# A hybrid decoder layer on one core: TensorE's order written out at two seams, after the recurrence and at attention's last head

## The chip, the cores and the metric

The kernel runs on one core of a Trainium2 chip. The time is the device time of one execution in microseconds (us); the figures given are medians of several executions. Five engines work side by side, each through its own list of instructions in order: TensorE (PE: products and transposes; its weight loads are shown as PEld), VectorE (DVE), ScalarE (ACT), GpSimd (POOL) and SyncE (SP), which issues most DMAs. They wait for one another by semaphores.

## The reference: what is computed

One layer of a decoder, 512 tokens of width 1024, all in float32:

```python
h    = rms_norm(x, norm_g)
proj = h @ w_in     # recurrence q, f, i and gate z_a; attention c_q, c_kv, rope key, gate z_b; merge gates
y_a  = hgrn2_branch(hq, hf, hi, hz, lb, hg_norm_g)   # 8 heads of 128, chunkwise gated recurrence,
                                                     # per-head rms_norm, * silu(z_a)
y_b  = mla_branch(cq, ckv, kr, mz, ...)              # 8 heads, latent attention: 128 plain + 64 rotated
                                                     # dimensions per key, causal softmax, * silu(z_b)
g    = sigmoid(glog + b_gate)
x    = x + (g[0] * (y_a @ w_proj_a) + g[1] * (y_b @ w_proj_b)) @ w_out
out  = rms_norm(x, final_norm_g)
```

## The kernel before

**Products.** Every large product is done as three products of rounded operands (`mm3`, lines 90 to 92): high x high, high x low, low x high. Each operand is therefore first split into a high half (a copy on ScalarE) and a low half (a subtraction on VectorE): weights in `load_w` (L111, L112), other operands in `split` (L149, L150). `proj_ch` projects 256 channels of `w_in` for all tokens: two weight halves `kh`, for each two groups of 128 channels `m`, for each four blocks `k`, that is 48 products of 128x512.

**Memory.** TensorE writes to PSUM. Of its eight banks the pool `mm` has three (projections) and the pool `ax` five (everything else: scores, states, outputs, transposes).

**Stages.** After the latent projections, the recurrence goes through its heads in four pairs (`hg_pair`). A pair projects the forget gate, the values or the output gate, and the query, then per head: `hg_states` (transposes L487, copy L488 to `kt`, products L492, VectorE L493 and L496), `hg_scores` (L504, L509, L512, then a masked copy L513 to `asb`), `hg_out` (L523, L525, then squares L529 on ScalarE, a power on GpSimd, L154 and L155, and the scaling L531 on VectorE into a buffer named `k128`), and `hg_gate` (transposes L539, then L540 into `ya`).

In the last pair two pieces of attention are written in between: `before_gate` does `mla_rope(0)` and `mla_nope(0)`, and `before_out` does `mla_scores(0)`, ahead of `hg_out`. Then comes `mla_gate(0)` (24 products on `hT`), and last `finish()`, which is `hg_gate` of both heads.

`mla_rope` makes the rotated query: a projection, a copy to `qr` (L598), DMAs that swap its halves (L600), three GpSimd operations (L601 to L603), a second pair of DMAs that exchanges the partition halves (L607), a rounding copy (L609) and a subtraction into `qp` (L613). `mla_nope` makes the plain query and key. `mla_scores` goes through four blocks of 128 queries; in each it issues

```python
mm3(sps[:, :n], qn, kn, ...)                                        # plain part, 3 products
for x in range(2):
    nc.tensor.matmul(sps[:, :n], qh[:, bl], kpe[x][:, :n], ...)     # rotated part, L658
```

and then the softmax (L661 to L666) into `p`. `mla_transpose` turns `p` by ten transposes (L679) and splits it into `pt`; `mla_out` multiplies it with the values and the result with the gate `z` (L689).

The loop over attention's heads does, for the next head ahead of time, the scores, gate and projections. At the last head it projects the first merge gates (`gates(0, 0)`: 48 products and two activations L698), then transposes, and after the loop comes `mla_out`. The merge follows: `parts` splits `ya` (eight copies on ScalarE, eight subtractions on VectorE), and `proj_ch` multiplies it with `w_proj_a`.

**Order.** Nearly all of the order is made by a planner: it takes the instructions in the order in which they are written as their priority, runs a time model of the engines, and writes down for each engine a fixed list. The engines then run these lists as they are. Only the start of the kernel is in a `tc.manual_schedule` block, in which the named engines keep the written order. `tc.issue_after(ins)` puts what is issued inside it on the engine of `ins` behind `ins` in that engine's list; before, the splitting of `ya` on ScalarE stands behind the last exponential of the last head (`last_exp`).

Of the kernel before, what the change touches and what calls it, by code (L numbers as in the profile page):

```python
# [13 lines left out]
AF = mybir.ActivationFunctionType  # L14
# [5 lines left out]
D = 1024  # L20
# [3 lines left out]
H = 8  # L24
# [3 lines left out]
COL_G = COL_ZB + 1024  # L28
# [10 lines left out]
def hybrid_layer(ctx: ExitStack, tc: tile.TileContext, a):  # L39
    nc = tc.nc  # L40
# [76 lines left out]
        v = mat[:, c0 : c0 + w].rearrange("(k p) c -> p k c", p=P)  # L117
        return [load_w(v[:, 4 * i : 4 * i + 4, :]) for i in range(2)]

    def proj_ch(mat, c0, rhs):  # L120

        ps = [mm_tile() for _ in range(2)]
        for kh, w in enumerate(load_cols(mat, c0)):
            for m in range(2):
                for k in range(4):
                    kk = 4 * kh + k
                    mm3(ps[m][:], w, rhs, (slice(None), k, slice(m * P, m * P + P)),
                        (slice(None), kk), kk == 0, kk == KD - 1)
        return ps

    def proj_tok(mat, c0, lhs, done):
# [3 lines left out]
        for t2 in range(NT // 2):  # L135
# [8 lines left out]
            for t in range(2):  # L144
                done(2 * t2 + t, ps[t])

    def split(hi, lo, src):

        nc.scalar.copy(hi, src)  # L149
        nc.vector.tensor_tensor(lo, src, hi.bitcast(F32), op=ALU.subtract)  # L150

    def power(out, x, mul, add, expo):
# [346 lines left out]
    def hg_scores(h, ki, ko, k64, qi, q64):  # L499

        asb, aps = asb_[h % 2], ax_tile()
        for i in range(NT):
            b = slice(i * P, i * P + P)
            nc.tensor.matmul(aps[:, b], ki[:, b], qi[:, b], start=True, stop=True)  # L504

        for c in (0, 2):
            for i in range(NT):
                blk = lambda n: slice(i * P + n * C, i * P + n * C + C)
                nc.tensor.matmul(aps[c * C : c * C + C, blk(c + 1)], ko[:, blk(c)], qi[:, blk(c + 1)], start=True, stop=True)  # L509
        for i in range(NT):  # L510
            b = slice(i * 64, i * 64 + 64)
            nc.tensor.matmul(aps[0:64, i * P + 64 : i * P + P], k64[:, b], q64[:, b], start=True, stop=True)  # L512
        nc.vector.copy_predicated(asb[:].rearrange("p (g t) -> p g t", g=NT),  # L513
                                  mask_le[:].rearrange("p (o t) -> p o t", o=1).broadcast_to([P, NT, P]),
                                  aps[:].rearrange("p (g t) -> p g t", g=NT))
        return asb

    def hg_out(h, asb, st_, q128, v_sb):

        ops = ax_tile()  # L520
        for i in range(NT):
            sl = slice(i * P, i * P + P)
            nc.tensor.matmul(ops[:, sl], asb[:, sl], v_sb[i][:, (h % 4) * P : (h % 4) * P + P], start=True, stop=i == 0)  # L523
            if i:
                nc.tensor.matmul(ops[:, sl], q128[:, sl], st_[:, i * P - P : i * P], start=False, stop=True)  # L525
        ss, on = W("ss", 2, (P, NT)), W("k128")
        for i in range(NT):
            osq = W("osq", 1, (P, P))
            nc.scalar.activation(osq[:], ops[:, i * P : i * P + P], AF.Square, accum_out=ss[:, i : i + 1])  # L529
        power(ss[:], ss[:], 1.0 / P, 4 * EPS, neg_half)  # L530
        nc.vector.tensor_tensor(on[:].rearrange("p (g v) -> p g v", g=NT), ops[:].rearrange("p (g v) -> p g v", g=NT),  # L531
                                ss[:].rearrange("p (g o) -> p g o", o=1).broadcast_to([P, NT, P]), op=ALU.mult)
        return on
# [12 lines left out]

    v_sb = [None] * NT

    def hg_pair(pair, before_gate=None, before_out=None):
        cc, hs = pair * 256, (2 * pair, 2 * pair + 1)  # L550
        pf = proj_ch(w_in, COL_F + cc, hT)
        kk = [hg_forget(h, pf[i]) for i, h in enumerate(hs)]
        def gate():
            pz = proj_ch(w_in, COL_ZA + cc, hT)
            zz = [z_tile() for _ in hs]
            for i in range(2):
                silu2(zz[i][:], pz[i][:])
            return zz

        if pair % 2 == 0:  # L560
            for t in range(NT):
                v_sb[t] = hw.tile([P, 512], F32, f"v{t}")
            proj_tok(w_in, COL_I + cc, hT, lambda t, ps: nc.scalar.copy(v_sb[t][:], ps[:]))
        else:
            zz = gate()
        pq = proj_ch(w_in, COL_Q + cc, hT)
        qq = [hg_query(h, pq[i], kk[i][0]) for i, h in enumerate(hs)]
        sts = [hg_states(h, kk[i][5], kk[i][1], v_sb) for i, h in enumerate(hs)]
        if before_gate:
            before_gate()  # L570
        if pair % 2 == 0:
            zz = gate()
        aa = [hg_scores(h, kk[i][2], kk[i][3], kk[i][4], qq[i][0], qq[i][1]) for i, h in enumerate(hs)]
        if before_out:
            before_out()
        on = [hg_out(h, aa[i], sts[i], qq[i][2], v_sb) for i, h in enumerate(hs)]

        def finish():
            for i, h in enumerate(hs):
                hg_gate(h, on[i], zz[i])  # L580
        return finish

    w_uq = a["w_uq"][0].rearrange("(k p) (h c) -> p k h c", p=P, h=H)
# [51 lines left out]
    def mla_gate(h):  # L637
        w = load_w(w_in[:, COL_ZB + h * P : COL_ZB + h * P + P].rearrange("(k p) c -> p k c", p=P))
        ps = mm_tile()
        for k in range(KD):  # L640
            mm3(ps[:], w, hT, (slice(None), k), (slice(None), k), k == 0, k == KD - 1)
        z = z_tile()
        silu2(z[:], ps[:])
        return z

    last_exp = [None]

    def mla_scores(h, pool, qn, kn, qp, final=False):

        pn = []  # L650
        for i in range(NT):
            n = (i + 1) * P
            bl = slice(i * P, n)
            sps = ax_tile()
            qh = qp[h % 2]
            mm3(sps[:, :n], qn, kn, (slice(None), bl), (slice(None), slice(0, n)), True, False)
            for x in range(2):
                nc.tensor.matmul(sps[:, :n], qh[:, bl], kpe[x][:, :n], start=False, stop=x == 1)  # L658
            sm = pool.tile([P, 4], F32, "sm", 4)
            p = pool.tile([P, n], F32, f"p{i}")  # L660
            nc.vector.tensor_tensor(sps[:, bl], sps[:, bl], mask_inf[:], op=ALU.add)  # L661
            nc.vector.tensor_reduce(sm[:, 0:1], sps[:, :n], axis=AX.X, op=ALU.max, negate=True)
            nc.vector.tensor_scalar(sm[:, 1:2], sm[:, 0:1], SCALE, None, op0=ALU.mult)  # L663
            last_exp[0] = nc.scalar.activation(p[:, :n], sps[:, :n], AF.Exp, scale=SCALE, bias=sm[:, 1:2], accum_out=sm[:, 2:3])  # L664
            nc.vector.reciprocal(sm[:, 3:4], sm[:, 2:3])
            (nc.vector if final else nc.gpsimd).tensor_scalar(p[:, :n], p[:, :n], sm[:, 3:4], 0.5, op0=ALU.mult, op1=ALU.mult)  # L666
            pn.append(p)
        return pn
# [15 lines left out]
    def mla_out(h, pts, v, z):  # L684
        ops = mm_tile()
        for j in range(NT):
            mm3(ops[:, j * P :], v, pts[j], (slice(None), j, slice((h % 4) * P, (h % 4) * P + P)), (slice(None),),
                j == 0, j == NT - 1)
        nc.vector.tensor_tensor(yb[:, h], ops[:], z[:], op=ALU.mult)  # L689


    def gates(b, c):

        res = []
        for i, ps in enumerate(proj_ch(w_in, COL_G + b * D + c * 256, hT)):
            j = 8 * b + 2 * c + i
            g = z_tile()
            nc.scalar.activation(g[:], ps[:], AF.Tanh, scale=0.5, bias=hb_gate[:, j : j + 1])  # L698
            res.append(g)
        return res  # L700

    for pair in range(H // 2 - 1):
        hg_pair(pair)()
    early = []

    def first_scores():
        early.append(mla_rope(0))
        early.append(mla_nope(0, ma_pool))

    finish = hg_pair(H // 2 - 1, first_scores, lambda: early.append(mla_scores(0, ma_pool, *early[1], early[0])))  # L710
    z = mla_gate(0)
    finish()
    hw.close()

    mw = Pool("mla", "right")
# [4 lines left out]
    for h in range(H):  # L720
        pools = (ma_pool, mw)
        if h:
            pn = mla_scores(h, pools[h % 2], *nope, qp, h + 1 == H)
        if h + 1 < H:
            if h % 2:
                qp = mla_rope((h + 1) // 2)
        if h:
            z = mla_gate(h)
        if h + 1 < H:
            nope = mla_nope(h + 1, pools[(h + 1) % 2])  # L730
        if late:
            mla_out(*late)
        if h % 4 == 0:
            v = mla_values(h)
        hook = lambda: mla_transpose(pn)
        if h + 1 == H:
            first_gates = gates(0, 0)
            pts = hook()
        else:
            pts = hook()  # L740
        late = (h, pts, v, z)
    mla_out(*late)
    mw.close()
    ma_pool.close()
    cpool.close()
# [11 lines left out]
    mp = Pool("merged", "right")  # L757
    ma = mp.tile([P, KD, S], F32, "ma")
    yap = Pool("ya_parts", "right")
    with tc.issue_after(last_exp[0].ins):  # L760
        yas = parts(yap, ya, "ya")
    for c in range(4):
        for i, (g, ps) in enumerate(merge(0, c, yas, a["w_proj_a"][0], None if c else first_gates)):
# [109 lines left out]
```

## Time and profile before

| | |
|---|---|
| time, median of 3 | 641.39 us (640.81 to 641.47) |
| the profiled execution | 641.92 us, its span 640.1 us |
| TensorE busy | 624.4 us (98%) |
| VectorE, ScalarE, GpSimd busy | 354.3, 238.9, 114.9 us |
| mean granted clock of TensorE | 0.991 |
| waits of TensorE for L531 and for `pt` | 3.4 us in two, 2.3 us in one |

The profile is of one execution. "Busy" of TensorE is modelled from pipelined instructions. The granted clock is the share of full speed that the chip gave TensorE in a stretch. In the lists of instructions a row has the start, the duration, the engine, the line, the operation, the output and inputs by their names, their shapes, and in brackets how long the engine had been idle before and what ended that.

### The profile page before, as it was taken

Reading aid. Unit: us, or ns where it says so; the run is one execution under the profiler, and the core shown is the slowest. Engines: PE = TensorE matmul, PEld = TensorE weight load, DVE = VectorE, ACT = ScalarE, POOL = GpSimd, SP = SyncE. Lnnn points to the kernel's source line nnn. Section 1 sums busy time; section 2 is a strip of 40 time slices with the busy share of each in tenths; the row PEclk is TensorE's granted clock in tenths of the full one; section 3 lists DMA queues with packets and bytes.
Section 4 is the critical chain, followed back from the end, with each engine's and each line's share of the span. In section 5 each row is a group of like instructions: output and inputs, shape, how many; then the busy total and the mean of one; then the engine's idle time right before and its main releaser. Section 6 shows DMA issues by size and latency. Waiting matters only on the chain.

```text
span 640.1 us, 8392 instructions
## 1 busy us (share of the span) xinstructions
PE 624.4 (98%) x3204; PEld 525.4 (82%) x3204; DVE 354.3 (55%) x552; ACT 238.9 (37%) x451; POOL 114.9 (18%) x213
## 2 busy tenths in 40 slices
PE   8999999999999999979999999989999999999995
PEld 5998888888888888868888888878888888888884
DVE  7727855497944478567567756556322342434244
ACT  5554241333242232355445645344222232323223
POOL 3106200332401033231213141000000010111011
PEclk9999999999999999999999999989999999999998
DMA  7425153133124103411332243123332323334403
GB/s 258 139 66 177 34 165 99 33 90 108 34 69 129 46 23 97 120 33 52 90 95 71 54 141 89 34 66 93 102 85 91 101 89 100 99 98 155 175 10 122
DMA packets 58808, 59.75 MB, mean 93 GB/s; under 512 B 5736, under 2 KB 52238, under 8 KB 58768
## 3 DMA queue, kind: packets, MB, share of 16 engines
q1 hardware_dynamic: 56492, 55.54, 28.9%
q10 hardware_dynamic: 2132, 3.15, 1.7%
q8 instruction: 25, 0.41, 0.3%
q0 software_dynamic: 144, 0.52, 0.3%
q14 instruction: 15, 0.12, 0.1%
HBM read 55.01 MB, written 2.10 MB: 89 GB/s over the span
## 4 chain that ended last, share of the span: by engine, by line
PE 95%; DVE 2%; ACT 1%; issue 0%; DMA 0%; POOL 0%; POOLq 0%; DVEq 0%; ACTq 0%
PE mm_ps L90 26%; PE mm_ps L92 26%; PE mm_ps L91 25%; PE ax_ps L90 2%; PE ax_ps L92 2%; PE ax_ps L91 2%; PE ax_ps L658 2%; PE ax_ps L679 2%; PE mm_ps L260 1%; PE ax_ps L504 1%; PE ax_ps L523 1%; PE ax_ps L492 1%; PE ax_ps L512 1%; PE ax_ps L525 1%; PE ax_ps L539 1%; PE ax_ps L509 1%
## 5 line engine op out<-in xcount | busy, mean ns | idle before, releaser
L112 DVE TENSOR_TENSOR w_lo<-w_raw,w_hi 128x1024 fp32r<-128x1024 f32 (+3 forms) x90 | 108.9, 1213 | 129.8 <-ACT w_hi L111 128.4
L111 ACT CAST w_hi<-w_raw 128x1024 fp32r<-128x1024 f32 (+3 forms) x90 | 89.3, 995 | 175.5 <-PE mm_ps L91 124.6
L90 PE MATMUL mm_ps<-hT,w_hi 128*128 128x512 f32 x384 | 150.6, 393 | 0.0
L91 PE MATMUL mm_ps<-hT,w_hi 128*128 128x512 f32 x384 | 149.9, 390 | 0.0
L92 PE MATMUL mm_ps<-hT,w_lo 128*128 128x512 f32 x384 | 149.3, 391 | 0.0
L92 PEld LDWEIGHTS mm_ps<-hT,w_lo 128*128 128x128 f32 x384 | 72.1, 188 | 14.8
L91 PEld LDWEIGHTS mm_ps<-hT,w_hi 128*128 128x128 f32 x384 | 72.1, 188 | 14.5
L90 PEld LDWEIGHTS mm_ps<-hT,w_hi 128*128 128x128 f32 x384 | 72.2, 188 | 14.3
L774 POOL TENSOR_TENSOR ma<-ma,z 128x512 f32<-128x512 f32 x8 | 11.8, 1480 | 181.1 <-DVE z L773 181.1
L91 PE MATMUL mm_ps<-w_lo,hT 128*128 128x512 f32 (+1 forms) x96 | 36.5, 382 | 0.0
L92 PE MATMUL mm_ps<-w_hi,hT 128*128 128x512 f32 (+1 forms) x96 | 36.4, 382 | 0.0
L90 PE MATMUL mm_ps<-w_hi,hT 128*128 128x512 f32 (+1 forms) x96 | 36.4, 386 | 0.0
L666 POOL TENSOR_SCALAR p<-p,sm 128x128 f32<-128x128 f32 (+3 forms) x28 | 16.9, 605 | 81.9 <-DVE sm L663 73.7
L449 DVE RECIPROCAL tf<-pr 128x512 f32<-128x512 f32 x8 | 26.8, 3349 | 0.2
L664 ACT ACTIVATE p<-ax_ps,sm 128x128 f32<-128x128 f32 (+3 forms) x32 | 16.9, 529 | 26.6 <-DVE sm L663 26.5
L91 PE MATMUL mm_ps<-ya,w_hi 128*128 128x512 f32 x64 | 25.7, 402 | 0.0
L92 PE MATMUL mm_ps<-ya,w_lo 128*128 128x512 f32 x64 | 25.6, 399 | 0.0
L90 PE MATMUL mm_ps<-ya,w_hi 128*128 128x512 f32 x64 | 25.5, 398 | 0.0
L90 PE MATMUL mm_ps<-yb,w_hi 128*128 128x512 f32 x64 | 24.9, 389 | 0.0
L91 PE MATMUL mm_ps<-yb,w_hi 128*128 128x512 f32 x64 | 24.9, 389 | 0.0
L92 PE MATMUL mm_ps<-yb,w_lo 128*128 128x512 f32 x64 | 24.9, 389 | 0.0
L150 DVE TENSOR_TENSOR wo<-wo_raw,wo 128x1024 fp32r<-128x1024 f32 x8 | 9.6, 1224 | 25.9 <-ACT wo L149 25.9
(226 smaller groups left out, 1124.6 us busy)
## 6 DMA issues: line engine op xcount, KB each, us to landing
w_raw<-w_in SPq DMA_DIRECT2D x58, 512.0 KB, 3.9
w_raw<-w_proj_a SPq DMA_DIRECT2D x8, 512.0 KB, 3.4
w_raw<-w_proj_b SPq DMA_DIRECT2D x8, 512.0 KB, 3.3
wo_raw<-w_out SPq DMA_DIRECT2D x8, 512.0 KB, 3.4
xr<-x SPq DMA_DIRECT2D x4, 512.0 KB, 7.7
w_raw<-w_in SPq DMA_DIRECT2D x4, 448.0 KB, 4.7
x<-x SPq DMA_DIRECT2D x3, 512.0 KB, 8.4
w_raw<-w_uq SPq DMA_DIRECT2D x8, 192.0 KB, 2.7
```

Source lines behind the costliest of these rows:

```text
L90: nc.tensor.matmul(ps, lh[lsl], rh[rsl], start=start, stop=False)
L91: nc.tensor.matmul(ps, lh[lsl], rl[rsl], start=False, stop=False)
L92: nc.tensor.matmul(ps, ll[lsl], rh[rsl], start=False, stop=stop)
L111: nc.scalar.copy(hi[:, :o], raw[:, :o])
L112: (lo_eng or nc.vector).tensor_tensor(lo[:, :o], raw[:, :o], hi[:, :o].bitcast(F32), op=ALU.subtract)
L150: nc.vector.tensor_tensor(lo, src, hi.bitcast(F32), op=ALU.subtract)
L449: nc.vector.reciprocal(rp[:], pr[:])
L658: nc.tensor.matmul(sps[:, :n], qh[:, bl], kpe[x][:, :n], start=False, stop=x == 1)
L664: last_exp[0] = nc.scalar.activation(p[:, :n], sps[:, :n], AF.Exp, scale=SCALE, bias=sm[:, 1:2], accum_out=sm[:, 2:3])
L666: (nc.vector if final else nc.gpsimd).tensor_scalar(p[:, :n], p[:, :n], sm[:, 3:4], 0.5, op0=ALU.mult, op1=ALU.mult)
L679: nc.tensor.transpose(tps[b][:, c : c + P], pn[i][:, j * P : j * P + P], ident[:])
L774: nc.gpsimd.tensor_tensor(ma[:, j], ma[:, j], g[:], op=ALU.add)
```

## The change

TensorE's order is written out in two places. First, the last pair of the recurrence gets a function `last`, which in a `manual_schedule` block for TensorE alone issues the scores of both heads, `hg_out` of both, `mla_scores(0)`, `mla_gate(0)` and the transposes of `hg_gate`. Second, at attention's last head the block holds the merge gates' projection, into which a hook puts the transposes of `p` ahead of its last 12 products (`kh` = 1, `m` = 1), and then `mla_out`. Third, the splitting of `ya` on ScalarE stands behind the last copy made by `split`, which is the last part of `pt`, and no more behind the last exponential. Inside a block only TensorE's instructions keep the written order; where instructions from outside fall among them is still the planner's choice, as are the other engines' lists.

```diff
-    def proj_ch(mat, c0, rhs):
+    def proj_ch(mat, c0, rhs, hook=None):
...
             for m in range(2):
+                if hook and kh and m:
+                    hook()
                 for k in range(4):
...
+    last_split = [None]
+
     def split(hi, lo, src):
 
-        nc.scalar.copy(hi, src)
+        last_split[0] = nc.scalar.copy(hi, src)
...
-    def hg_pair(pair, before_gate=None, before_out=None):
+    def hg_pair(pair, before_gate=None, last=None):
...
-        aa = [hg_scores(h, kk[i][2], kk[i][3], kk[i][4], qq[i][0], qq[i][1]) for i, h in enumerate(hs)]
-        if before_out:
-            before_out()
-        on = [hg_out(h, aa[i], sts[i], qq[i][2], v_sb) for i, h in enumerate(hs)]
-
-        def finish():
+        def scores():
+            return [hg_scores(h, kk[i][2], kk[i][3], kk[i][4], qq[i][0], qq[i][1]) for i, h in enumerate(hs)]
+
+        def outs(aa):
+            return [hg_out(h, aa[i], sts[i], qq[i][2], v_sb) for i, h in enumerate(hs)]
+
+        def gated(on):
             for i, h in enumerate(hs):
                 hg_gate(h, on[i], zz[i])
-        return finish
-
+
+        if last:
+            return last(scores, outs, gated)
+        gated(outs(scores()))
...
-    def gates(b, c):
+    def gates(b, c, hook=None):
 
         res = []
-        for i, ps in enumerate(proj_ch(w_in, COL_G + b * D + c * 256, hT)):
+        for i, ps in enumerate(proj_ch(w_in, COL_G + b * D + c * 256, hT, hook)):
...
-    finish = hg_pair(H // 2 - 1, first_scores, lambda: early.append(mla_scores(0, ma_pool, *early[1], early[0])))
-    z = mla_gate(0)
-    finish()
+    def last_outputs(scores, outs, gated):
+
+        with tc.manual_schedule(engines={mybir.EngineType.PE}):
+            on = outs(scores())
+            early.append(mla_scores(0, ma_pool, *early[1], early[0]))
+            z = mla_gate(0)
+            gated(on)
+        return z
+
+    z = hg_pair(H // 2 - 1, first_scores, last_outputs)
...
         if h + 1 == H:
-            first_gates = gates(0, 0)
-            pts = hook()
+            with tc.manual_schedule(engines={mybir.EngineType.PE}):
+                pts = []
+                first_gates = gates(0, 0, lambda: pts.extend(hook()))
+                mla_out(h, pts, v, z)
         else:
-            pts = hook()
-        late = (h, pts, v, z)
-    mla_out(*late)
+            late = (h, hook(), v, z)
...
-    with tc.issue_after(last_exp[0].ins):
+    with tc.issue_after(last_split[0].ins):
         yas = parts(yap, ya, "ya")
```

More of the change, by code (lines that the diff above doesn't have):

```diff
@@ L644, in mla_gate @@
         return z
-    last_exp = [None]
     def mla_scores(h, pool, qn, kn, qp, final=False):
@@ L663, in mla_scores @@
             nc.vector.tensor_scalar(sm[:, 1:2], sm[:, 0:1], SCALE, None, op0=ALU.mult)
-            last_exp[0] = nc.scalar.activation(p[:, :n], sps[:, :n], AF.Exp, scale=SCALE, bias=sm[:, 1:2], accum_out=sm[:, 2:3])
+            nc.scalar.activation(p[:, :n], sps[:, :n], AF.Exp, scale=SCALE, bias=sm[:, 1:2], accum_out=sm[:, 2:3])
             nc.vector.reciprocal(sm[:, 3:4], sm[:, 2:3])
@@ L702, in hybrid_layer @@
     for pair in range(H // 2 - 1):
-        hg_pair(pair)()
+        hg_pair(pair)
     early = []
```

## The prediction

> **What bounds the kernel now.** I read the page first: shares, then the chain that ended last.
>
> ```profile
> span 640.1 us, 8392 instructions
> ...
> PE 624.4 (98%) x3204; PEld 525.4 (82%) x3204; DVE 354.3 (55%) x552; ACT 238.9 (37%) x451; POOL 114.9 (18%) x213
> ...
> PE 95%; DVE 2%; ACT 1%; issue 0%; DMA 0%; POOL 0%; POOLq 0%; DVEq 0%; ACTq 0%
> ```
>
> TensorE is busy nearly always and carries the end. The change removes no product, so it can only win back time in which TensorE stands still or runs slowly. Its waits come next (us in total, times, longest), then a table by stretch (PE, PEld, DVE, ACT, POOL busy, granted clock, DMA share, GB/s).
>
> ```profile
> PE ax_ps L539 <- DVE k L531: 3.4, 2, 1.9
> PE mm_ps L90 <- ACT pt L149: 2.3, 1, 2.3
> ...
> 284.20:287.60 3.40, 0.66 (x4) 0.42 (x4) 1.86 (x3) 2.12 (x9) 1.96 (x3) 0.97 0.26 58
> 287.60:291.00 3.40, 3.17 (x16) 3.17 (x17) 2.19 (x5) 1.27 (x3) 0.00 (x0) 0.53 0.02 5
> ...
> 420.60:424.00 3.40, 1.31 (x6) 1.06 (x7) 3.40 (x5) 2.80 (x6) 0.00 (x0) 0.99 0.32 95
> 424.00:427.40 3.40, 3.40 (x10) 2.69 (x9) 0.39 (x1) 0.00 (x0) 0.00 (x0) 0.51 0.70 213
> ```
>
> The first wait is the recurrence's end (3.4 us before the transposes of L539), the second the last head (2.3 us before its output product). Behind each, one stretch of 3.4 us runs at half clock. That costs 0.47 x 3.17 = 1.5 us at the first place and 0.49 x 3.40 = 1.7 at the second. So the first loses 3.4 + 1.5 = 4.9 us, the second 2.3 + 1.7 = 4.0; 8.9 us is the most that the change can bring.
>
> **The recurrence's end.** Added: a written order on TensorE (scores of both heads, both `hg_out`, scores of attention head 0, its gate, the transposes). Moved: `hg_out` ahead of attention's scores, and all 24 products of `mla_gate(0)` behind them. First what cover the gate gives now, and when the inputs of the moved products are there.
>
> ```profile
> 259.58 0.83 PE L492 MATMUL ax_ps<-v,kt 128*128 128x128 f32 x6
> 260.25 0.49 PE L487 MATMUL ax_ps<-ident,k 128*128 128x128 f32 x3
> ...
> 261.96 0.39 PE L90 MATMUL mm_ps<-hT,w_hi 128*128 128x512 f32 x1
> ...
> 266.49 0.83 PE L492 MATMUL ax_ps<-v,kt 128*128 128x128 f32 x6
> 267.16 1.06 PE L504 MATMUL ax_ps<-qi,ki 128*128 128x128 f32 x8
> ...
> 271.49 0.33 PE L90 MATMUL ax_ps<-kn,qn 128*128 128x128 f32 x1
> ...
> 271.88 0.33 PE L90 MATMUL ax_ps<-kn,qn 128*128 128x256 f32 x1
> ...
> 281.84 0.39 PE L92 MATMUL mm_ps<-w_hi,cT 128*128 128x512 f32 x1
> ...
> 282.06:283.80 1.74, 1.73 (x15) 1.00 0.00 0
> ...
> 250.24 0.69 DVE L467 TENSOR_TENSOR k<-ko,gh 128x512 f32<-128x512 f32 x1
> 261.05 0.48 ACT L488 COPY kt<-ax_ps 128x384 f32<-128x384 f32 x1 [1.97 <-PE ax_ps L487]
> 264.31 1.28 POOL L601 TENSOR_TENSOR qr<-qr,qtab 128x512 f32<-128x512 f32 x1 [5.58 <-DMA qs<-qr]
> 268.21 1.17 ACTq L607 DMA_DIRECT2D qs<-qr  x2
> 272.20 0.62 ACT L609 CAST qh<-qs 128x512 fp32r<-128x512 f32 x1 [1.54 <-DMA qs<-qr]
> 272.86 1.40 DVE L613 TENSOR_TENSOR qp<-qs,qh 64x512 fp32r<-64x512 f32 x2 [0.51 <-ACT qh L609]
> ```
>
> (The stretch from 282.06 is one head's `hg_out`.) From 261.96 to 266.49 TensorE does 20 of the gate's 24 products, 0.227 us each, though `kt` is there at 261.53 and L492 could run. These 4.5 us now move behind the scores, so the work before attention's scores runs earlier:
> - L492 from 261.96: 266.49 to 267.16, 0.67 us.
> - Scores of both heads: 267.16 to 271.49, 4.33 us.
> - Two `hg_out`: 2 x 1.73 = 3.46 us.
> - The three latent products of the first block: 271.49 to 271.88, 0.39 us.
>
> Sum 8.85: TensorE stands at the first product with the rotated query (L658) at 270.81. That query does not depend on TensorE any more. It comes by a DMA, three GpSimd products, a second pair of DMAs issued by ScalarE at 268.21, the cast of L609 and the subtraction of L613, whose first half ends at 272.86 + 0.70 = 273.56. `mla_scores` writes three latent and two rotated products block by block, and the order written out now holds the other blocks' latent products behind the first L658. **New wait: 273.6 - 270.8 = 2.8 us**; behind it stand the rest of the scores, the gate and the transposes.
>
> Could other products fill it? Those of the next head's queries and values (on `cT`) need a PSUM tile of the pool `mm`, after the gate's in writing order. The planner seems to hand out a pool's tiles strictly in that order: `k` of L467 is there at 250.93, four of the five `ax` tiles are free, and yet L487 of that head starts only behind L492 of the head before, at 260.25. The gate's tile is taken when its first product may go, behind the scores. So I take no filler: 2.8 us. The ends are 0 (a filler is found) and 2.8 plus what ScalarE's queue adds.
>
> The clock: both idle times before (3.4 us in two parts, 2.3 in one) were followed by a half-clock stretch, so I add the mean of 1.5 and 1.7: 1.6 us; the ends are 0 and 1.7. [...]
>
> What the old waits turn into: the normalised output of L531 waits for these rows now.
>
> ```profile
> 283.88 0.28 ACT L529 ACTIVATE osq<-ax_ps 128x128 f32<-128x128 f32 x1 [0.70 <-PE ax_ps L525]
> ...
> 285.82 1.01 POOL L155 TENSOR_TENSOR ss<-ss,fixed 128x4 f32<-128x4 f32 x1
> ...
> 287.09 0.68 DVE L531 TENSOR_TENSOR k<-ax_ps,ss 128x512 f32<-128x512 f32 x1
> 287.83 1.11 PE L539 MATMUL ax_ps<-ident,k 128*128 128x128 f32 x4 [1.44 <-DVE k L531]
> ```
>
> From the first square (283.88) to the transposes (287.83) that is 4 us. In the new order `hg_out` ends at 270.4, so even with 3 us lost on ScalarE behind exponentials it is ready by 278. The gate ends at 273.6 + 2.9 (rest of the scores) + 1.6 + 24 x 0.227 = 283.5. The wait of 3.4 us goes, with 5 us to spare; without the gate it would be back. The fourth block needs the PSUM tile of the first `hg_out`, which L531 frees at about 275, when the third block runs: 0, at most 1 us. The weight loads on SP keep their order, and the gate's weights hold their slot some 9 us longer: 0, since the next gate comes 15 us later.
>
> First place: 4.9 before, 2.8 + 1.6 = 4.4 after. **Gain 0.5 us.**
>
> **The last head.** Moved: the ten transposes ahead of the gate's last 12 products, the output product behind them, and the eight conversions of `ya` behind the last copy of `pt` on ScalarE.
>
> ```profile
> 419.13 1.25 PE L679 MATMUL ax_ps<-ident,p 128*128 128x128 f32 x10
> 422.69 0.50 PE L90 MATMUL mm_ps<-pt,v 128*128 128x512 f32 x1 [2.30 <-ACT pt L149]
> ...
> 414.86 4.25 ACT L149 CAST ya<-ya 128x512 fp32r<-128x512 f32 x8
> 419.02 1.04 ACT L111 CAST w_hi<-w_raw 128x1024 fp32r<-128x1024 f32 x1
> ...
> 421.48 0.69 ACT L698 ACTIVATE z<-mm_ps,hb_gate 128x512 f32<-128x512 f32 x1
> 422.06 1.34 ACT L149 CAST pt<-ax_ps 128x512 fp32r<-128x512 f32 x3
> ...
> 415.29 0.49 DVE L666 TENSOR_SCALAR p<-p,sm 128x512 f32<-128x512 f32 x1
> 415.69 4.89 DVE L150 TENSOR_TENSOR ya<-ya,ya 128x512 fp32r<-128x512 f32 x8
> 422.78 1.61 DVE L150 TENSOR_TENSOR pt<-ax_ps,pt 128x512 fp32r<-128x512 f32 x3
> ```
>
> ScalarE reaches `pt` at 422.06 only, behind `ya`, two weight casts and both gate activations. In the new order (in the old run's times) the transposes start 12 x 0.227 = 2.7 us earlier, at 416.4, which is 0.6 behind the last `p` (415.78), and end at 417.65. Twelve products reach to 420.4. The copies, at worst behind one weight cast and all behind the last transpose, end at 417.65 + 1.04 + 1.34 = 420.0; the low halves follow one by one. The output product does not wait. It takes 3 x 0.227 x (1 + 0.75 + 0.5 + 0.25) = 1.7 us (512 down to 128 columns), so `ya` is wanted at 422.1. Its conversion starts at 419 to 420 and takes 0.53 on ScalarE and 0.61 on VectorE a piece; VectorE is through with `pt` at 421, and the first piece is there at 421.6. TensorE takes 3 x 0.227 = 0.68 a piece, so the rest keeps ahead. Cost 0, with 0.5 us to spare; if that cover fails, `ya` is late next. **Gain 4.0 us** (0 to 4.0).
>
> **Sum.** 0.5 + 4.0 = 4.5 us. The profiled execution took 641.92 us (span 640.1), 0.5 above the median of 641.39; from the median, 636.9.
>
> **The rivals.**
> - **Both waits go**: the planner finds cover for the 2.8 us. For it: `cT` products filled other places of this stretch (the row at 281.84); against it the tile order above. 641.4 - 8.9 = 632.5.
> [...]
> - **The second wait comes back**: ScalarE still puts weight casts and activations ahead of `pt`, and `ya` behind it. 640.9. Against it: `pt` is ready earlier and written earlier.
> - **Slower: ScalarE's queue holds up the rotated query.** `hg_out` now ends soon after the DMA issue of L607 (268.21), and its squares may be listed ahead of it (four take at most 1.9 us, from 283.88 to the L155 row at 285.82). Eight end at 272.3; with two weight casts of 1.04 the issue moves from 268.21 to 274.4, the wait from 2.8 to 9.0 us: 9.0 + 1.6 = 10.6 against 4.9, and 4.0 won: 641.4 + 5.7 - 4.0 = 643.1. It decides if the issue comes 4.5 us late, after 272.7. Against it: L607 can go at 268.2, before the first `hg_out` ends at 268.7.
>
> **How the numbers follow.** As forecast 0.43 (own range 635.8 to 638.5), clock holds 0.13, both waits go 0.20, second wait back 0.13, slower 0.11. The likeliest gives 636.9. The two rivals below reach to 632.5; the second wait back must be taken in too, or 0.24 is left out: 632.4 to 641.0 leaves out 0.11. A change of 0.2% (1.3 us) is about what can be told from none: faster 0.76, same 0.13, slower 0.11.
>
> **What would show it.** Right: L658 of head 0 waits about 2.8 us for DVE L613, a half-clock stretch follows, and neither L539 nor the last head's L90 appears among the waits. The first place is misjudged if products on `cT` stand between `hg_out` and L658, or if L658 doesn't wait. The last head is wrong if TensorE waits for ACT `pt` or `ya`. All of it is wrong if the planner's new order opens a wait elsewhere, where there is none now.

## The result and the profile after

| | before | after |
|---|---|---|
| time, median | 641.43 us (640.81 to 642.29, 4 runs) | 636.58 us (635.34 to 636.87, 4 runs) |
| the profiled execution | 641.92 us, span 640.1 | 636.65 us, span 634.9 |
| mean granted clock | 0.991 | 0.995 |

The ratio is 0.992, with a 95% interval of 0.9902 to 0.9937: 4.85 us gained, where 4.5 were forecast (636.9 us). The lines of the changed kernel have moved by four to seven: L492 is now L496, L525 is L529, L529 is L533, L531 is L535, L539 is L543, L607 is L614, L609 is L616, L613 is L620, L658 is L664, L679 is L685, L149 is L153.

The page of the changed kernel: span, busy time of TensorE, and the shares of the chain that ended last.

```profile
span 634.9 us, 8391 instructions
...
PE 622.2 (98%) x3204; PEld 524.1 (83%) x3204; DVE 353.0 (56%) x552; ACT 239.7 (38%) x451; POOL 114.5 (18%) x213
...
PE 94%; DMA 2%; DVE 1%; ACT 1%; POOL 1%; ACTq 0%; issue 0%; SPq 0%; POOLq 0%
```

TensorE still carries the end, and its busy time has fallen by 2.2 us although it does the same 3204 products. By the account below, 1.5 us of that are the clock (3.2 us lost before, 1.7 after). The list of its waits has lost both old entries, and has one new one:

```profile
PE ax_ps L664 <- DVE qp L620: 2.2, 1, 2.2
```

**The recurrence's end.** The instructions of this stretch on TensorE (the first row stands where the gate's products stood), then ScalarE and VectorE, in order of time, and below them the table by stretch (PE, PEld, DVE, ACT, POOL busy, granted clock, DMA share, GB/s).

```profile
262.41 0.83 PE L496 MATMUL ax_ps<-v,kt 128*128 128x128 f32 x6
...
270.83 0.28 PE L92 MATMUL ax_ps<-kn,qn 128*128 128x128 f32 x1
273.32 0.44 PE L664 MATMUL ax_ps<-kpe,qp 128*128 128x128 f32 x2 [2.22 <-DVE qp L620]
...
283.25 1.03 PE L543 MATMUL ax_ps<-ident,k 128*128 128x128 f32 x8
```

```profile
268.98 1.17 ACTq L614 DMA_DIRECT2D qs<-qr  x2
...
271.46 0.28 ACT L533 ACTIVATE osq<-ax_ps 128x128 f32<-128x128 f32 x1
...
271.93 0.62 ACT L616 CAST qh<-qs 128x512 fp32r<-128x512 f32 x1
...
272.58 1.40 DVE L620 TENSOR_TENSOR qp<-qs,qh 64x512 fp32r<-64x512 f32 x2 [4.32 <-ACT qh L616]
...
276.72 0.68 DVE L535 TENSOR_TENSOR k<-ax_ps,ss 128x512 f32<-128x512 f32 x1
```

```profile
270.50:273.90 3.40, 1.18 (x10) 1.04 (x10) 1.29 (x2) 3.26 (x13) 0.20 (x1) 0.98 0.24 54
...
273.32:280.12 6.80, 6.80 (x28) 6.09 (x29) 5.37 (x18) 3.81 (x17) 4.01 (x7) 0.75 0.00 1
```

TensorE stands still for 2.2 us at the first product with the rotated query, between the last plain product of the first block and the first half of L620. From there it is busy for 6.8 us without a gap, and yet gets 0.75 of the clock: 0.25 x 6.80 = 1.7 us lost, which is one stretch of 3.4 us at half clock (in slices of 0.85 us: 0.86 from 273.15, 0.50 from 274.00 to 276.55, 0.63 behind that). The transposes L543 no longer wait: the last scaling L535 ends at 277.4, the gate's products at 283.25.

**The last head.** First TensorE, then ScalarE.

```profile
415.34 1.25 PE L685 MATMUL ax_ps<-ident,p 128*128 128x128 f32 x10
416.35 0.48 PE L90 MATMUL mm_ps<-hT,w_hi 128*128 128x512 f32 x1
...
419.18 0.39 PE L90 MATMUL mm_ps<-pt,v 128*128 128x512 f32 x1
...
419.86 0.39 PE L90 MATMUL mm_ps<-ya,w_hi 128*128 128x512 f32 x1
```

```profile
416.12 0.85 ACT L153 CAST pt<-ax_ps 128x512 fp32r<-128x512 f32 x2
416.85 0.64 ACT L153 CAST ya<-ya 128x512 fp32r<-128x512 f32 x1
417.37 0.61 ACT L153 CAST pt<-ax_ps 128x512 fp32r<-128x512 f32 x1
417.85 3.76 ACT L153 CAST ya<-ya 128x512 fp32r<-128x512 f32 x7
```

No row of TensorE has an idle time in brackets. ScalarE makes its three copies of `pt` from 416.12 to 417.98, the last one ending 1.4 us behind the transposes (416.59), with one piece of `ya` between (the copy after which `ya` may go is the last one written, and the planner had put that one second of the three).

### The profile page after: what moved, and what is told of

Read it like the earlier page. It is cut to its first block, busy times and chain, and to the rows that moved or that the text cites. A ratio compares the mean times of both kernels' runs of the same rounds, so it can differ in the third digit from the quotient of the medians.

```text
span 634.9 us, 8391 instructions
## 1 busy us (share of the span) xinstructions
PE 622.2 (98%) x3204; PEld 524.1 (83%) x3204; DVE 353.0 (56%) x552; ACT 239.7 (38%) x451; POOL 114.5 (18%) x213
## 4 chain that ended last, share of the span: by engine, by line
PE 94%; DMA 2%; DVE 1%; ACT 1%; POOL 1%; ACTq 0%; issue 0%; SPq 0%; POOLq 0%
PE mm_ps L90 26%; PE mm_ps L91 26%; PE mm_ps L92 26%; PE ax_ps L91 2%; PE ax_ps L90 2%; PE ax_ps L92 2%; PE ax_ps L664 2%; PE mm_ps L264 1%; PE ax_ps L685 1%; DMA w_raw<-w_in 1%; PE ax_ps L508 1%; PE ax_ps L527 1%; PE ax_ps L529 1%; PE ax_ps L496 1%; PE ax_ps L516 1%; PE ax_ps L543 1%
## 5 line engine op out<-in xcount | busy, mean ns | idle before, releaser
L672 POOL TENSOR_SCALAR p<-p,sm 128x128 f32<-128x128 f32 (+3 forms) x28 | 15.3, 548 | 79.4 <-DVE sm L671 47.5
L91 PE MATMUL mm_ps<-ya,w_hi 128*128 128x512 f32 x64 | 25.0, 390 | 0.0
L90 PE MATMUL mm_ps<-ya,w_hi 128*128 128x512 f32 x64 | 24.8, 389 | 0.0
```

What stands on the lines that cost most here:

```text
L90: nc.tensor.matmul(ps, lh[lsl], rh[rsl], start=start, stop=False)
L91: nc.tensor.matmul(ps, lh[lsl], rl[rsl], start=False, stop=False)
```

## The experiments

In all of them two questions are kept apart by place: how long TensorE stands still there, and what the stretch behind it loses to the clock. The clock loss is an estimate from a table row that starts where the idle time ends: (1 - granted clock) x its length.

**1. Each half alone.** `only_recurrence` undoes the last head's part, `only_last_head` the recurrence's.

```diff
# only_recurrence, against the changed kernel
-            with tc.manual_schedule(engines={mybir.EngineType.PE}):
-                pts = []
-                first_gates = gates(0, 0, lambda: pts.extend(hook()))
-                mla_out(h, pts, v, z)
+            first_gates = gates(0, 0)
+            pts = hook()
...
-    with tc.issue_after(last_split[0].ins):
+    with tc.issue_after(last_exp[0].ins):
```

```diff
# only_last_head, against the changed kernel
-        with tc.manual_schedule(engines={mybir.EngineType.PE}):
-            on = outs(scores())
-            early.append(mla_scores(0, ma_pool, *early[1], early[0]))
-            z = mla_gate(0)
-            gated(on)
+        aa = scores()
+        early.append(mla_scores(0, ma_pool, *early[1], early[0]))
+        on = outs(aa)
+        z = mla_gate(0)
+        gated(on)
```

> Has the hand order of the recurrence's end alone; the last head, its transposes and the ya copies are as before. Theory (the traces of before and after compared: the old end lost 3.4 us idle and 1.5 us of half clock, the new one loses 2.2 us idle and 1.6 us of half clock): gain 1.1 us, so a ratio near 0.998 (0.9975 to 0.9995), about 640.4 us where before has 641.4; the last head's wait for pt and the slow stretch behind it are there as before. Rival: the recurrence's end carries most of the gain, ratio 0.995 or less (638 us).

> Has the last head's order and the ya copies behind pt alone; the recurrence's end is as before. Theory: gain 4.0 us (2.3 us idle and 1.7 us of half clock go), ratio near 0.9938, about 637.4 us; at the recurrence's end the wait of the transposes for DVE's k stays at about 3.2 us with its slow stretch. Rival: the gain was mostly the recurrence's end, and this one has 639.5 us or more.

Measured: `only_last_head` 637.70 us, ratio 0.9937 (0.9924 to 0.9950), as expected; its waits show 3.4 us before L543 (the first row below) and none at the last head. `only_recurrence` 637.68 us, ratio 0.9936 (0.9924 to 0.9949): more than three times the expected gain. That is the time of its rival, but the rival put the gain at the recurrence's end, and it lies at the last head. Either half alone gains 3.8 us, and both together 4.85. The wait of `only_last_head`, the waits of `only_recurrence`, then the latter's last head on ScalarE and TensorE, and the table by stretch:

```profile
PE ax_ps L543 <- DVE k L535: 3.4, 2, 1.9
...
PE ax_ps L665 <- DVE qp L621: 2.2, 1, 2.2
...
PE mm_ps L90 <- ACT pt L154: 0.9, 1, 0.9
```

```profile
411.09 0.69 ACT L671 ACTIVATE p<-ax_ps,sm 128x512 f32<-128x512 f32 x1 [0.69 <-DVE sm L670]
...
411.77 4.26 ACT L154 CAST ya<-ya 128x512 fp32r<-128x512 f32 x8
...
418.02 1.25 PE L686 MATMUL ax_ps<-ident,p 128*128 128x128 f32 x10
...
419.57 1.34 ACT L154 CAST pt<-ax_ps 128x512 fp32r<-128x512 f32 x3
```

```profile
420.19:426.99 6.80, 6.79 (x33) 5.78 (x33) 1.68 (x4) 0.72 (x2) 0.00 (x0) 1.00 0.47 144
```

The recurrence's place behaves as in the changed kernel. What differs is the last head, whose code is that of before: its wait is 0.9 us instead of 2.3, and no half clock follows. The planner makes one list for the whole kernel, and with the new end of the recurrence it has put the last head's scores earlier among the other products: behind them and the values' products, 30 gate products stand ahead of the transposes, where before has 21. The last exponential starts at 411.09, 6.9 us ahead of the transposes. In before the same row was

```profile
414.19 0.69 ACT L664 ACTIVATE p<-ax_ps,sm 128x512 f32<-128x512 f32 x1 [0.62 <-DVE sm L663]
```

and the transposes at 419.13, 4.9 us apart. ScalarE has the same eight copies, two weight casts and two activations to do between exponential and `pt`, and 2 us more for them. So 2.3 + 1.7 us of loss became 0.9, without an edit at that place. The gains of the two halves overlap: the edit at the last head is worth 3.8 us on the old list and 1.1 us on this one.

**2. What stands in the new wait.** `gate_first` issues the gate ahead of attention's scores; `gate_split1` only its first three products; `gate_tile_ax` leaves the written order and takes the gate's PSUM tile from the other pool.

```diff
# gate_first, against the changed kernel
             on = outs(scores())
-            early.append(mla_scores(0, ma_pool, *early[1], early[0]))
             z = mla_gate(0)
+            early.append(mla_scores(0, ma_pool, *early[1], early[0]))
             gated(on)
```

```diff
# gate_split1: the scores are issued inside the gate, ahead of its k step 1
+            if between and k == first:
+                between()
             mm3(ps[:], w, hT, (slice(None), k), (slice(None), k), k == 0, k == KD - 1)
...
-            early.append(mla_scores(0, ma_pool, *early[1], early[0]))
-            z = mla_gate(0)
+            z = mla_gate(0, 1, lambda: early.append(mla_scores(0, ma_pool, *early[1], early[0])))
```

```diff
# gate_tile_ax
-        ps = mm_tile()
+        ps = tile()
...
-            z = mla_gate(0)
+            z = mla_gate(0, ax_tile)
```

> The changed kernel with mla_gate(0) issued ahead of mla_scores(0) in the hand-ordered block. Theory: the 24 gate products (5.4 us) stand where TensorE waited 2.2 us for the rotated query; wait and half-clock stretch go, worth 2.2 + 1.6 = 3.8 us: about 632.8 us, ratio near 0.9866 to before, no wait named L664 and the granted clock at 1.00 in the stretch. Rival 1: the transposes L543, now only some 20 cT products and four score blocks behind the recurrence's outputs, wait for the normalised outputs again, 1 us or more: 634 us or above. Rival 2: the scores come 5.4 us later, the softmax chain behind them is late, and head 0's transposes wait: 634 us or above with that wait in the list.

> The changed kernel, but of the 24 gate products only the first 3 (0.7 us, one of 8 k steps) are issued ahead of the scores, so that the gate's PSUM tile is handed out ahead of them; the other 21 stay behind. Theory (tiles are handed out in written order, so a tile taken early lets the planner put the next head's cT products into the wait): the whole wait of 2.2 us and the half clock behind it go although only 0.7 us of the gate moved: 633.2 us (632.7 to 634.5). Rival (only the moved products cover): wait 1.5 us left, 635.9 us, or 634.4 us if the clock holds.

> The changed kernel with its order of source, but mla_gate(0) takes its PSUM tile from the pool ax instead of mm. Theory (the prediction's claim that the gate's mm tile, handed out in written order behind the scores, keeps all later mm products from filling the wait): with the mm tiles free, the next head's cT products stand ahead of the first rotated product, the 2.2 us wait for the rotated query goes and the half clock with it: 632.8 us (632.3 to 634.0). Rival: the wait stays since nothing else is ready, 636.6 us.

Measured: `gate_first` 633.14 us (632.82 to 633.33), ratio 0.9870 (0.9855 to 0.9884); `gate_split1` 633.73 us, 0.9876 (0.9863 to 0.9889); `gate_tile_ax` 634.54 us, 0.9891 (0.9874 to 0.9907), half a microsecond over its expected range, while the first two came as forecast. In none of them does TensorE wait for the rotated query. TensorE in `gate_split1`, where the wait was:

```profile
270.20 0.47 PE L90 MATMUL mm_ps<-hT,w_hi 128*128 128x512 f32 x1
...
271.15 0.28 PE L92 MATMUL ax_ps<-kn,qn 128*128 128x128 f32 x1
271.26 0.45 PE L90 MATMUL mm_ps<-cT,w_hi 128*128 128x512 f32 x1
...
274.51 0.39 PE L92 MATMUL mm_ps<-cT,w_lo 128*128 128x512 f32 x1
274.73 0.33 PE L666 MATMUL ax_ps<-kpe,qp 128*128 128x128 f32 x2
```

Three gate products moved, and fifteen products of the next head on `cT` now stand ahead of the first rotated one. They were ready in the changed kernel too (their weights are split by 257.2 there), and were not used. The only thing that the edit frees is the gate's PSUM tile, handed out before the scores instead of behind them; `gate_tile_ax` frees the `mm` tiles in another way, with the same effect at this place. So the prediction's claim holds: the planner hands out a pool's tiles in written order, and a tile that is asked for behind a waiting product keeps all later work of its pool behind it.

The table by stretch of `gate_first`:

```profile
270.50:277.30 6.80, 6.80 (x37) 5.81 (x36) 2.77 (x5) 5.97 (x21) 2.59 (x4) 1.00 0.11 25
283.00:289.80 6.80, 6.50 (x39) 5.41 (x37) 5.80 (x11) 4.72 (x12) 1.28 (x2) 1.00 0.14 31
```

No idle time and full clock where 2.2 + 1.7 us were lost; neither rival (L543 or the softmax late) came. What is left is 0.3 us behind the transposes. `gate_first` beats both kernels: 8.4 us under before, 3.4 under the changed one. The profiled execution of `gate_tile_ax` is 1.2 us longer than that of `gate_first`. Most of it is idle time soon after, 1.2 us against 0.3, and the longest piece is a wait for an `ax` tile, of which the gate now holds one:

```profile
PE ax_ps L90 <- DVE ya L544: 0.8, 1, 0.8
```

`gate_split1`, whose gate holds no `ax` tile, has 0.3 us of the same wait.

**3. What of the last head's part does it.** `only_ya_late` moves only the copies of `ya`; `last_head_ya_early` moves only the transposes. Both have the recurrence's end as before.

```diff
# only_ya_late, against before
-    with tc.issue_after(last_exp[0].ins):
+    with tc.issue_after(last_split[0].ins):
```

```diff
# last_head_ya_early, against only_last_head
-    with tc.issue_after(last_split[0].ins):
+    with tc.issue_after(last_exp[0].ins):
```

> The kernel before with one edit: the copies of ya are issued behind a copy of pt; the last head's transposes stay behind the gate products, and the recurrence's end is as before. Theory (ScalarE's queue made the wait: in the trace of before the 8 ya copies, 4.25 us, the weight copies and the two gate activations stand between the last exponential and pt): without the ya copies ScalarE reaches pt near the end of the transposes, the wait for pt falls from 2.3 us to 0.3 to 0.9 us, no half-clock stretch follows, gain 3.1 to 3.7 us: 638.1 us (637.6 to 638.8). Rival: without the 12 gate products behind the transposes the wait stays above 1.5 us with its slow stretch, 640 us or more.

> Like the run with the last head's order alone (637.7 us there), but the ya copies stay where before has them, behind the last exponential and ahead of pt. Theory: transposes end near 417.5 and 12 gate products cover to 420.2; ScalarE does ya to about 419.1, one gate activation and the first copy of pt to 420.5, so a wait of 0.3 to 1.2 us and no slow stretch: 638.4 us (637.9 to 639.2). Rival 1: the place of the transposes alone does it, 637.7 us with no wait. Rival 2: the wait comes back at 2 us with its slow stretch, 640.5 us or more.

Measured: `last_head_ya_early` 638.65 us, 0.9956 (0.9943 to 0.9968), in its range, but with no wait at the last head, as its first rival had it: ScalarE reaches `pt` at 420.08, and TensorE's gate products last to 420.71.

```profile
420.08 1.34 ACT L154 CAST pt<-ax_ps 128x512 fp32r<-128x512 f32 x3
...
420.71 0.50 PE L90 MATMUL mm_ps<-pt,v 128*128 128x512 f32 x1
```

So the transposes' place alone takes the wait away. The copies' place is not free all the same: this kernel is 0.95 us slower than `only_last_head`, and each of its five executions is slower than all six of that one. Two of its five executions, 639.04 and 639.47, have a mean clock of 0.992, the others, among them the profiled one, 0.994. What the two lose, and where, stays open. `only_ya_late` took 640.31 us, 0.9978 (0.9969 to 0.9987): 2.2 us above the forecast. That is the time of its rival, but not for the rival's reason: at its own place it is nearly as expected in the profile.

```profile
PE mm_ps L90 <- ACT pt L153: 0.9, 1, 0.9
...
PE mm_ps L90 <- ACT ya L153: 0.3, 1, 0.3
```

1.2 us of waits instead of 2.3, and the stretch of 6.8 us from 422.78 runs at 1.00 of the clock. Part of the rest is lost elsewhere: at the recurrence's end, which the edit does not touch, the profile has the same 3.4 us of waits as before, and then 0.55 of the clock over 6.8 us, that is 3.1 us lost instead of 1.5. This execution, 640.99 us, is the slowest of the twelve; five took 639.7 to 639.9, and one 638.55 at a mean clock of 0.998, near the forecast.

**4. The clock.** That asked for second profiles of three kernels, and for a wait cut in length. `plain_first` issues the plain products of blocks 1 and 2 ahead of the first rotated one.

```diff
# plain_first, against the changed kernel
+        for i in range(ahead):
+            start(i)          # plain products of block i
         for i in range(NT):
...
-            early.append(mla_scores(0, ma_pool, *early[1], early[0]))
+            early.append(mla_scores(0, ma_pool, *early[1], early[0], ahead=3))
```

> The changed kernel, but in the first attention head the products of kn with qn of score blocks 1 and 2 (0.9 us in sum) are issued ahead of the rotated products of block 0, so they lie inside the wait for the rotated query, which falls from 2.2 us to about 1.3 us. What is asked is the clock: after 0.9 us of idle (last head, recurrence part alone) it stayed at 1.00, after 2.2 us it fell to half for 3.4 us. Theory: 1.3 us is too short, the slow stretch goes: 634.1 us (633.6 to 634.6) and the groups of runs at two times go with it. Rival: any wait over 1 us halves it: 635.7 us.

> The kernel of the run only_ya_late once more, for a second profile. Its twelve times lay in groups (638.6; 639.7 to 639.9; 640.7 to 641.0), and its first profile, 641.0 us, has 6.8 us at half clock behind the recurrence's two waits of 3.4 us in sum, where before, with the same products there, has 3.4 us. Theory (behind the same idle the stretch at half clock is there or not, and once or twice, from execution to execution): if this execution takes 639.8 or less, its stretch there is 3.4 us or none, with waits of the same length as before. Rival: the groups have another cause; then the profile shows 6.8 us at half clock whatever the time, or waits of another length.

> The kernel before once more, for a second profile: its first, 641.9 us, has one stretch of 3.4 us at half clock at each of the two places. Theory: an execution of 640.4 to 641.0 lacks one of the two stretches (1.7 us) with the waits unchanged at 3.4 and 2.3 us; one of 642 has both. Rival: the faster ones have shorter waits and both stretches.

> The changed kernel once more, for a second profile: its first, 636.65 us, waits 2.2 us at the first rotated product and then has 3.4 us at half clock. Theory: an execution near 635.3 has the same wait of 2.2 us and no stretch at half clock, one near 636.6 has both. Rival: the wait itself differs between the two.

`plain_first`: 637.19 us, 0.9926 (0.9914 to 0.9938), worse than either theory. The first wait is 1.3 us as planned, but a second one follows, for the PSUM tile of block 3, which is now the first block's and is free only behind its exponential:

```profile
PE ax_ps L90 <- ACT p L680: 1.3, 1, 1.3
PE ax_ps L674 <- DVE qp L620: 1.3, 1, 1.3
```

With 2.6 us idle in two pieces the half clock is there in the profiled execution:

```profile
275.32:282.12 6.80, 6.80 (x23) 5.46 (x24) 2.94 (x12) 2.02 (x6) 3.01 (x5) 0.75 0.00 1
```

One of the other five executions took 635.42 us at a mean clock of 0.999, 1.7 us less than the profiled one. Whether one wait of 1.3 us would bring it is not answered by this run.

The second profiles settle the other question. `only_ya_late_2` took 639.98 us, `before_2` 640.89, `after_2` 636.62 (again 2.2 us of wait and a half-clock stretch, so it adds nothing). First the recurrence's end in `only_ya_late` and in `only_ya_late_2`, then the last head in before and in `before_2`, each from the end of the same wait (3.4 us in two pieces; 2.3 us):

```profile
287.88:294.68 6.80, 6.79 (x26) 6.09 (x27) 4.07 (x7) 2.55 (x5) 0.00 (x0) 0.55 0.01 2
```

```profile
288.08:294.88 6.80, 6.79 (x34) 6.07 (x35) 4.76 (x8) 2.92 (x6) 0.00 (x0) 0.75 0.01 2
```

```profile
422.69:429.49 6.80, 6.80 (x23) 5.49 (x24) 1.70 (x4) 0.71 (x2) 0.00 (x0) 0.75 0.51 154
```

```profile
423.25:430.05 6.80, 6.80 (x33) 5.77 (x33) 1.69 (x4) 0.71 (x2) 0.00 (x0) 1.00 0.52 154
```

The same program with the same wait loses 3.1 us to the clock in one execution and 1.7 in another, or 1.7 and nothing. The times of a kernel with such waits lie in groups that fit this: before, in the 28 runs beside these experiments, 640.4 to 641.1 in ten and 642.0 to 642.4 in twelve, with mean clocks of 0.995 to 0.996 and of 0.991. Six lie between, at 0.993; no profile shows what those have.

**The account.** Each profiled execution, with its idle times at the two places and what the table rows give for the clock (us):

| kernel | time | recurrence's end: idle + clock | last head: idle + clock | what is left |
|---|---|---|---|---|
| before | 641.92 | 3.4 + 1.5 | 2.3 + 1.7 | 633.0 |
| before_2 | 640.89 | 3.4 + 1.7 | 2.3 + 0 | 633.5 |
| after | 636.65 | 2.2 + 1.7 | 0 | 632.8 |
| after_2 | 636.62 | 2.2 + 1.7 | 0 | 632.7 |
| only_recurrence | 637.83 | 2.2 + 1.7 | 0.9 + 0 | 633.0 |
| only_last_head | 637.76 | 3.4 + 1.7 | 0 | 632.7 |
| last_head_ya_early | 638.30 | 3.4 + 1.7 | 0 | 633.2 |
| only_ya_late | 640.99 | 3.4 + 3.1 | 1.2 + 0 | 633.3 |
| only_ya_late_2 | 639.98 | 3.4 + 1.7 | 1.2 + 0 | 633.7 |
| plain_first | 637.12 | 2.6 + 1.7 | 0 | 632.8 |
| gate_first | 633.33 | 0.3 + 0 | 0 | 633.0 |
| gate_split1 | 633.63 | 0.6 + 0 | 0 | 633.0 |
| gate_tile_ax | 634.56 | 1.2 + 0 | 0 | 633.4 |

Times from 633.3 to 641.9 come down to 632.7 to 633.7. So all else, in the edits or by chance, comes to 1.0 us at most between any two of these executions, and no row shows where that lies.

## Why the prediction was right, point by point

- **Sum.** Forecast 0.5 + 4.0; in the two profiled executions 4.9 - 3.9 = 1.0 and 4.0 - 0 = 4.0. The likeliest case came about; no rival did. That 636.9 lies so near the median of 636.6 is in part luck: the first place gave twice what was forecast, and losses read from an execution with the half clock at both places were taken off a median of executions that in part lack it at one. The two profiled executions differ by 5.3 us, the medians by 4.85.
- **The new wait** was forecast at 2.8 us and is 2.2. TensorE's arrival was right: 8.85 us behind the start of L492 forecast, 8.7 measured (262.41 to 271.1). The mis-sized term is the rotated query: forecast 11.6 us behind the same row, 10.9 measured (273.28 - 262.41). Its second pair of DMAs was issued 0.3 us later behind that row (6.57 us instead of 6.25), but landed in 2.3 us instead of 3.5; here are the issues in the stretch from 262 to 276, before and after:

```profile
qs<-qr ACTq DMA_DIRECT2D x2, 128.0 KB, 3.5
```

```profile
qs<-qr ACTq DMA_DIRECT2D x2, 128.0 KB, 2.3
```

The old landing time had been kept, though the work around these transfers moved. What made the difference was not tried.
- **No filler**: right, and shown by `gate_split1` and `gate_tile_ax`.
- **Half clock behind the wait**: forecast 1.6, measured 1.7 in both profiles of the changed kernel. That the clock holds, the case with a chance of 0.13 (1.6 us less), is not ruled out: of four times one was 635.34, at a mean clock of 0.997 against 0.994 to 0.995 for the others, and `before_2` has 1.00 behind a wait of 2.3 us. No profile of such an execution of the changed kernel was caught, and what decides between the two was not shown.
- **The old wait of L543** goes with time to spare: forecast ready by 278 against a gate that ends at 283.5; 277.4 and 283.25 measured. It is also what lets `gate_first` work, whose transposes come at 279.2 to 284.2.
- **ScalarE's queue** (the slower rival): one square (0.47 us with its read) slipped in ahead of the cast of L616, none ahead of the DMA issue. That rival needed eight.
- **The last head**: the gain of 4.0 was right against an execution with the half clock there, and is 2.3 against one without. The timing of `pt` was pessimistic: no weight cast stood ahead of it, and all three copies were done at 417.98, 2.6 us behind the start of the transposes, where 3.6 were forecast. `ya` was wanted sooner than forecast (0.7 us behind the first output product, not 1.7), and was there.
- **What the prediction did not see**: that the last head's loss hung on the list as a whole. It took the two places as separate; `only_recurrence` shows that the first edit alone would have removed 3.1 us of the second's 4.0. The sum came out right because the last head's part then took the rest.

## What to carry to other kernels

Where a planner hands out PSUM tiles in written order, an order written by hand decides not only what waits but also what may fill the wait: put work that is ready, or at least its first piece, ahead of the product whose input is late. Before a gain is summed over two places, look whether the first edit moves the list at the second. And compare kernels place by place, as idle time plus clock loss, since a median can mix executions with and without the half clock: behind the same wait of 2.3 us before has 0.75 of the clock over 6.8 us, and `before_2` 1.00.

## What the runs showed of the hardware

- Idle of 2.2 or 2.3 us was followed by 3.4 us at half clock in four profiles (before, after, after_2, only_recurrence: 0.75 of the clock over 6.8 us) and by none in one (before_2: 1.00); 0.9 us, or 0.9 and 0.3, by none in three (only_recurrence, only_ya_late, only_ya_late_2: 1.00); 2.6 us in two pieces by 3.4 us (plain_first: 0.75); 3.4 us in two pieces by 3.4 us in five profiles (0.75 to 0.78) and by 6.8 in one (only_ya_late: 0.55). One gap of 2.2 us cost 1.7 us of clock (after: 0.25 x 6.80). Why one program has the stretch in one execution and not, or twice as long, in another was not shown.
- A pair of DMAs of 128 KB each took 3.5 us to land in one surrounding (before) and 2.3 in the other (after), and the query that hangs on them came 0.7 us sooner behind the same row. Which part of the surroundings did it was not tried.
